# Rows of running sums fetched on GpSimd's queue instead of SyncE's, in a two-layer hybrid SSD and attention kernel

## The chip, the cores and the metric

The kernel runs on one core of one Trainium2 chip. The metric is the device time of one execution in microseconds (us), the median of several runs. An instruction that starts a DMA stands in the stream of the engine whose queue carries it: SyncE (SP) has no arithmetic and is used as a queue only, while GpSimd (POOL) both computes and issues.

## The reference, cut to what matters

Two layers of a parallel-branch block over 256 latent and 256 context tokens, model width 1024. Per layer:

```python
u_l = modulate(rmsnorm(xl, norm1_w[i]), sh1_l, sc1_l) @ w_in[i]     # and u_c for the context
ys  = ssd_branch(...)          # bidirectional Mamba-2 scan, 16 heads, chunks of 128 tokens
ya  = diff_attn_branch(...)    # differential attention, 8 heads
xl  = xl + g1_l * branch_merge(ys_l, ya_l, gate_l, w_br_ssd[i], w_br_att[i], w_out[i])
xl  = xl + g2_l * conv_ffn(h_l, w_up[i], ffn_conv_w[i], ffn_conv_b[i], w_down[i])
```

The part around the change is the scan inside a chunk, for each head and each of two directions:

```python
a_cs     = jnp.cumsum(a, axis=-1)              # running sums of dt * a_head
decay_in = jnp.exp(segsum(a))                  # exp(a_cs[l] - a_cs[s])
y_diag   = jnp.einsum('bgcls,bgrcls,bcsgrp->bclgrp', cb, decay_in, xd)
y_off    = jnp.einsum('bclgn,bcgrpn,bgrcl->bclgrp', cc, h_in, jnp.exp(a_cs))
```

## The kernel before, in words

All weights are float32 and stream from DRAM once per use. Tiles of 128 x 4 x 256 (`raw`, three buffers, 512 KB each) are loaded by `load_w` (L304) on SP's queue. ScalarE (ACT) rounds each to a high part `whi` (L313), VectorE (DVE) takes the remainder `wlo` (L314), three buffers each, and TensorE (PE) makes three matmuls of them (L393 to L395, L407 to L409). The order of instructions on each engine is chosen at build time by a scheduler from its own estimates; only attention and scan matmuls are pinned in program order. On the chip every engine works through its stream strictly in that order.

The scan's work is woven into the big matmuls: generators `states` and `outputs` (one of each for every group g of four heads) are advanced a step at a time by `pump` while the matmuls of xs (L1019 to L1021), the gates and z are emitted. The running sums are computed once per layer, and written by eight small DMAs to the DRAM tensor `csd` (L861). `outputs` then needs, for chunk t and group g, the sums of four heads and two directions spread over all 128 partitions. This is the tile `cs` (128 x 2 x 4 x 128, two buffers), which `fetch` (L950) fills with one broadcast DMA: rows of 2 KB from `csd`, the same to every partition, 512 KB in all. There are 16 fetches in layer 0 (four chunks) and 8 in layer 1 (two chunks), 24 together.

From a fetched `cs`, `head` makes what the chunk's matmuls need, in this order: ACT takes cc = exp(cs) (L966); POOL subtracts the column sums in place, once for each direction (L969, twice); DVE takes the minimum of the two directions (L972); ACT takes its exponential, E (L974); DVE multiplies cc by C (L975). Later DVE multiplies X by E (L993), which is the last reader of the `cs` buffer. A fetch for chunk t + 2 into the same buffer can go once that L993 is done. The first two fetches of a layer have no earlier `cs`: they wait for the memory of the attention branch, which is free when the last matmul of the GEMM with `w_br_att` has read `yah` (pmmmm<-yah,wlo).

POOL's other work here is `xd` (L925), the decayed inputs of the state matmuls `psstate` (L930). PE takes these in program order, so that everything behind one in PE's stream waits for it. xs of head pair j comes from two PSUM banks (`mm`) by a convolution (`conv3`: L568 on ACT, L571 and L572 on DVE), a tanh (L665) and a product (L666); PE then transposes xs (psssT). A bank can be written again after its L572.

```python
raw = fetch(0)
nxt = head(0, raw)
if NT > 1: raw = fetch(1)
for t in range(NT):
    ...                       # X of chunk t, times E (L993)
    if t + 1 < NT: nxt = head(t + 1, raw)
    if t + 2 < NT: raw = fetch(t + 2)
    ...                       # pyyd matmuls of chunk t
```

Of the kernel before, what the change touches and what calls it, by code (L numbers as in the profile page):

```python
# [59 lines left out]
def hybrid_backbone_kernel(  # L60
# [6 lines left out]
    nc = tc.nc  # L67
    V, A, G, T = nc.vector, nc.scalar, nc.gpsimd, nc.tensor
# [7 lines left out]
    def nm(s):  # L76
        cnt[0] += 1
        return f"{s}_{cnt[0]}"

    def bank(tag, what=""):  # L80
        return psp.tile([P, 512], F32, tag=tag, name=nm("p" + tag + what), bufs={"mm": 2, "s": 3, "y": 2, "m": 1}[tag])


    def pmm(*a, **k):
        return tc.keep_in_program_order(T.matmul(*a, **k))  # L85
# [489 lines left out]
    for i in range(DEPTH):  # L575
# [41 lines left out]
        if i == 0:  # L617
# [5 lines left out]
            for f in range(4):  # L623
# [10 lines left out]
                for cc in range(2):  # L634
                    for fb in range(2):
                        cs = slice(fb * P, fb * P + P)
# [182 lines left out]
        if True:  # L819
# [28 lines left out]
            for dr in range(2):  # L848
                cs = slice(16 * dr, 16 * dr + 16)
# [94 lines left out]
        def outputs(g, sh):  # L944
            while "xT" not in sh:
                yield None
            xT, h_in = sh["xT"], sh["h"]
            yb = [bank("y", "yd"), bank("y", "yd")]

            def fetch(t):  # L950
                cs = up.tile([P, 2, 4, P], F32, tag="cs", name=nm("cs"), bufs=2)
                nc.sync.dma_start(cs.rearrange("p d h l -> p d (h l)"),
                                  csd[t, :, 4 * g:4 * g + 4, :].rearrange("d h l -> d (h l)").partition_broadcast(P))
                return cs

            def head(t, cs):
                tsl = slice(t * P, (t + 1) * P)
                cb = bank("s", "cb")
                pmm(cb[:, 0:P], BF[g][:, tsl], CF[g][:, tsl], start=True, stop=True)
                cbm = up.tile([P, 2, P], F32, tag="cbm", name=nm("cbm"), bufs=2)  # L960
                V.tensor_tensor(cbm, cb[:, 0:P].unsqueeze(1).to_broadcast([P, 2, P]), tri2, op=ALU.mult)

                cc = up.tile([P, 2, 4, P], F32, tag="cc", name=nm("cc"), bufs=2)
                dirs = [dr for dr in range(2) if not (dr == 0 and t == 2) and not (dr == 1 and t == 3)]
                d0, d1 = dirs[0], dirs[-1] + 1
                A.activation(cc[:, d0:d1], cs[:, d0:d1], AF.Exp)  # L966

                for dr in range(2):
                    G.tensor_tensor(cs[:, dr], cs[:, dr],  # L969
                                    csc[:, t, 16 * dr + 4 * g:16 * dr + 4 * g + 4].unsqueeze(2).to_broadcast([P, 4, P]),  # L970
                                    op=ALU.subtract)
                V.tensor_tensor(cs[:, 0], cs[:, 0], cs[:, 1], op=ALU.min)  # L972
                E = cs[:, 1]
                A.activation(E, cs[:, 0], AF.Exp)  # L974
                V.tensor_tensor(cc[:, d0:d1].rearrange("p d h l -> p (d h) l"), cc[:, d0:d1].rearrange("p d h l -> p (d h) l"),  # L975
                                CF[g][:, tsl].unsqueeze(1).to_broadcast([P, 4 * (d1 - d0), P]), op=ALU.mult)
                return cbm, cc, E, dirs

            raw = fetch(0)
            yield 1  # L980
            nxt = head(0, raw)
            if NT > 1:
                raw = fetch(1)
            yield 1
            for t in range(NT):
                tsl = slice(t * P, (t + 1) * P)
                cbm, cc, E, dirs = nxt
                X = up.tile([P, 4, P], F32, tag="X", name=nm("X"), bufs=2)
                for h in range(4):
                    dcol = [dtT[:, t, 16 * dr + 4 * g + h:16 * dr + 4 * g + h + 1] for dr in range(2)]  # L990
                    A.activation(X[:, h, :], cbm[:, 0, :], AF.Copy, scale=dcol[0])
                    V.scalar_tensor_tensor(X[:, h, :], cbm[:, 1, :], dcol[1], X[:, h, :], op0=ALU.mult, op1=ALU.add)
                V.tensor_tensor(X, X, E, op=ALU.mult)  # L993
                yield 1
                if t + 1 < NT:
                    nxt = head(t + 1, raw)
                    yield 1
                if t + 2 < NT:
                    raw = fetch(t + 2)
                while "done" not in sh:  # L1000
                    yield None
                for f in range(2):
                    for h in (2 * f, 2 * f + 1):
                        r = slice(64 * (h % 2), 64 * (h % 2) + 64)
                        pmm(yb[f][r, tsl], xT[:, t, h * 64:(h + 1) * 64], X[:, h, :], start=True, stop=False)
                    for dr in dirs:
                        for h in (2 * f, 2 * f + 1):
                            r = slice(64 * (h % 2), 64 * (h % 2) + 64)
                            pmm(yb[f][r, tsl], h_in[dr, t][:, h * 64:(h + 1) * 64], cc[:, dr, h, :],
                                start=False, stop=dr == dirs[-1])  # L1010
                yield 1
            for f in range(2):
                j = 2 * g + f
                V.scalar_tensor_tensor(xs[j][:, 0:N], xs[j][:, 0:N], L["D"][:, j:j + 1], yb[f][:, 0:N],
                                       op0=ALU.mult, op1=ALU.add)
            done.append(g)
            yield 1
# [189 lines left out]
```

## Time and profile before

| | us |
|---|---|
| median of 3 runs (1746.28 to 1748.42) | 1747.45 |
| the profiled execution | 1740.01 |
| its span, first to last instruction | 1738.2 |
| PE busy in it | 1667.1 (96%) |
| DVE busy | 1148.0 (66%) |
| ACT busy | 848.2 (49%) |
| POOL busy | 181.3 (10%) |
| mean granted TensorE clock | 0.993 of full speed |

Rows of the profile name an engine, a line of the kernel, the operation and its tiles as output<-input. In a timeline a row starts with its start and its length in us, and ends with the idle time ahead of it and what ended that, in square brackets. In a list of waits the three numbers are the total, the number of waits and the longest. In a table of stretches the columns are the length, the busy time and count of each engine, the granted clock (PEclk, 1.00 is full speed), the share of the DMA engines and GB/s.

### The profile page before, as it was taken

Reading aid. Unit: us, or ns where it says so; the run is one execution under the profiler, and the core shown is the slowest. Engines: PE = TensorE matmul, PEld = TensorE weight load, DVE = VectorE, ACT = ScalarE, POOL = GpSimd, SP = SyncE. Lnnn points to the kernel's source line nnn. Section 1 sums busy time; section 2 is a strip of 40 time slices with the busy share of each in tenths; the row PEclk is TensorE's granted clock in tenths of the full one; section 3 lists DMA queues with packets and bytes.
Section 4 is the critical chain, followed back from the end, with each engine's and each line's share of the span. In section 5 each row is a group of like instructions: output and inputs, shape, how many; then the busy total and the mean of one; then the engine's idle time right before and its main releaser. Section 6 shows DMA issues by size and latency. Waiting matters only on the chain. (4 is left out here: it accounts for less than half of the span.)

```text
span 1738.2 us, 27022 instructions
## 1 busy us (share of the span) xinstructions
PE 1667.1 (96%) x10547; PEld 1406.2 (81%) x10547; DVE 1148.0 (66%) x2008; ACT 848.2 (49%) x1567; POOL 181.3 (10%) x212
## 2 busy tenths in 40 slices
PE   7999999999988999999999999999999898989997
PEld 4788878777766788888888888788879788989997
DVE  4776667325988855766666326666675789779964
ACT  3565665413545423644444225555655455466653
POOL 3000010001433000300000002100000252010000
PEclk9999999999999999999999999999999999989999
DMA  9644333555443234233323335844535445646653
GB/s 317 215 127 126 115 119 108 166 173 146 121 107 100 74 109 146 74 97 97 97 87 95 92 108 161 255 146 146 152 93 171 121 110 144 199 154 185 193 176 117
DMA packets 233199, 240.71 MB, mean 138 GB/s; under 512 B 10908, under 2 KB 223551, under 8 KB 233071
## 3 DMA queue, kind: packets, MB, share of 16 engines
q1 hardware_dynamic: 230720, 237.14, 45.4%
q8 instruction: 83, 1.36, 0.3%
q0 software_dynamic: 1312, 1.03, 0.2%
q10 hardware_dynamic: 1039, 0.81, 0.1%
q14 instruction: 45, 0.37, 0.1%
HBM read 234.62 MB, written 4.33 MB: 137 GB/s over the span
## 5 line engine op out<-in xcount | busy, mean ns | idle before, releaser
L314 DVE TENSOR_TENSOR wlo<-raw,whi 128x1024 fp32r<-128x1024 f32 (+1 forms) x318 | 388.3, 1221 | 255.7 <-ACT whi L313 254.8
L313 ACT CAST whi<-raw 128x1024 fp32r<-128x1024 f32 (+1 forms) x318 | 329.2, 1036 | 378.4 <-PE pmmmm L408 146.6
L407 PE MATMUL pmmmm<-th,whi 128*128 128x512 f32 x744 | 306.3, 412 | 1.6 <-DVE chv L572 1.6
L408 PE MATMUL pmmmm<-tl,whi 128*128 128x512 f32 x744 | 296.5, 399 | 0.0
L409 PE MATMUL pmmmm<-th,wlo 128*128 128x512 f32 x744 | 295.6, 397 | 0.0
L407 PEld LDWEIGHTS pmmmm<-th,whi 128*128 128x128 f32 x744 | 140.5, 189 | 42.2 <-issue 7.9
L409 PEld LDWEIGHTS pmmmm<-th,wlo 128*128 128x128 f32 x744 | 140.4, 189 | 34.5 <-issue 1.0
L408 PEld LDWEIGHTS pmmmm<-tl,whi 128*128 128x128 f32 x744 | 140.5, 189 | 31.0 <-issue 2.2
L393 PE MATMUL pmmmm<-th,whi 128*128 128x256 f32 x480 | 138.5, 289 | 1.5 <-ACT whi L313 1.3
L395 PE MATMUL pmmmm<-th,wlo 128*128 128x256 f32 x480 | 134.7, 281 | 0.6 <-DVE wlo L314 0.6
L394 PE MATMUL pmmmm<-tl,whi 128*128 128x256 f32 x480 | 134.8, 281 | 0.0
L969 POOL TENSOR_TENSOR cs<-cs,csc 128x512 f32<-128x512 f32 x48 | 69.1, 1454 | 264.0 <-DMA cs<-csd 141.5
L393 PEld LDWEIGHTS pmmmm<-th,whi 128*128 128x128 f32 x480 | 90.7, 189 | 6.2 <-issue 3.8
L394 PEld LDWEIGHTS pmmmm<-tl,whi 128*128 128x128 f32 x480 | 90.8, 189 | 0.7 <-issue 0.4
L395 PEld LDWEIGHTS pmmmm<-th,wlo 128*128 128x128 f32 x480 | 90.6, 189 | 0.8 <-DVE wlo L314 0.8
L409 PE MATMUL psmm<-th,wlo 128*128 128x512 f32 x200 | 79.3, 397 | 0.0
L725 ACT ACTIVATE e<-psscore,nmx 128x512 f32<-128x512 f32 (+1 forms) x96 | 58.1, 610 | 43.5 <-DVE nmx L722 40.5
L408 PE MATMUL psmm<-tl,whi 128*128 128x512 f32 x200 | 79.2, 396 | 0.0
L521 POOL TENSOR_TENSOR rs<-ms,mhalf 128x2 f32<-128x2 f32 x9 | 6.3, 699 | 698.5 <-DVE ms L518 698.5
L407 PE MATMUL psmm<-th,whi 128*128 128x512 f32 x200 | 79.0, 395 | 0.0
L722 DVE TENSOR_REDUCE nmx<-psscore 128x1 f32<-128x512 f32 (+1 forms) x80 | 51.8, 684 | 34.3 <-PE psscore L85 34.2
L441 PE MATMUL pmmmm<-whi,th 128*128 128x256 f32 x256 | 74.3, 290 | 0.0
(346 smaller groups left out, 3899.0 us busy)
## 6 DMA issues: line engine op xcount, KB each, us to landing
raw<-in_w_in_dram SPq DMA_DIRECT2D x124, 512.0 KB, 4.0
raw<-in_w_up_dram SPq DMA_DIRECT2D x88, 512.0 KB, 3.6
mraw<-in_w_mod_dram SPq DMA_DIRECT2D x80, 512.0 KB, 4.7
raw<-in_w_down_dram SPq DMA_DIRECT2D x45, 512.0 KB, 3.6
cs<-csd SPq DMA_DIRECT2D x24, 512.0 KB, 5.8
boot<-in_w_mod_dram SPq DMA_DIRECT2D x16, 512.0 KB, 9.3
raw<-in_w_br_att_dram SPq DMA_DIRECT2D x16, 512.0 KB, 3.6
raw<-in_w_br_ssd_dram SPq DMA_DIRECT2D x16, 512.0 KB, 3.5
```

The costliest lines, as they stand in the source:

```text
L313: pin(A.copy(hi[:, 0:n, :], raw[:, 0:n, :]))
L314: pin(V.tensor_tensor(lo[:, 0:n, :], raw[:, 0:n, :], hi[:, 0:n, :].bitcast(F32), op=ALU.subtract))
L393: T.matmul(o[f], whi[:, kk, cs], xh, start=first, stop=False)
L394: T.matmul(o[f], whi[:, kk, cs], xl, start=False, stop=False)
L395: T.matmul(o[f], wlo[:, kk, cs], xh, start=False, stop=last)
L407: T.matmul(o, whi[:, k % 4, cs], hi[k][:, 0:n], start=k == 0, stop=False)
L408: T.matmul(o, whi[:, k % 4, cs], lo[k][:, 0:n], start=False, stop=False)
L409: T.matmul(o, wlo[:, k % 4, cs], hi[k][:, 0:n], start=False, stop=k == k_tiles - 1)
L441: T.matmul(b[:, n, :], hi[k][:, ts], whi[:, k % 4, :], start=k == 0 and n == 0, stop=False)
L722: V.tensor_reduce(nmx[:, cc, 0:ng], sc[cc].rearrange("p (g k) -> p g k", g=ng), axis=AX.X, op=ALU.max, negate=True)
L725: A.activation(e[cc][:, g * w:(g + 1) * w], sc[cc][:, g * w:(g + 1) * w], AF.Exp, bias=nmx[:, cc, g:g + 1], accum_out=sm[:, cc, g:g + 1])
L969: G.tensor_tensor(cs[:, dr], cs[:, dr], csc[:, t, 16 * dr + 4 * g:16 * dr + 4 * g + 4].unsqueeze(2).to_broadcast([P, 4, P]), op=ALU.subtract)
```

## The change

One line: the DMA in `fetch` is issued by GpSimd (`G`) instead of SyncE.

```diff
             def fetch(t):
                 cs = up.tile([P, 2, 4, P], F32, tag="cs", name=nm("cs"), bufs=2)
-                nc.sync.dma_start(cs.rearrange("p d h l -> p d (h l)"),
+                G.dma_start(cs.rearrange("p d h l -> p d (h l)"),
                                   csd[t, :, 4 * g:4 * g + 4, :].rearrange("d h l -> d (h l)").partition_broadcast(P))
                 return cs
```

SP's stream loses its 24 fetches, and otherwise keeps its order. POOL's stream gains them, and the scheduler, which now counts on the fetches at other times, puts some work of ACT, DVE, PE and POOL in another order near them. Three places matter below. In the pieces, a minus marks a row that stands there before and a plus one that stands there now.

First, ACT at the start of the scan of layer 0. `cs_4044` and `cs_4067` are the first two fetched tiles, `chv_3939` is the convolution of the first half of xs, `whi_3979` and `whi_3997` are the weights of the next matmuls.

```order
 L313 CAST whi_3909<-raw_3889 128x1024
-L568 ACTIVATE chv_3939<-pmmmm_3913,cols_157 128x512
-L665 ACTIVATE cth_3938<-chv_3939 128x512
-L313 CAST whi_3979<-raw_3895 128x1024
 L966 ACTIVATE cc_4060<-cs_4044 128x1024
 L966 ACTIVATE cc_4109<-cs_4067 128x1024
+L974 ACTIVATE cs_4044<-cs_4044 128x512
+L568 ACTIVATE chv_3939<-pmmmm_3913,cols_157 128x512
+L974 ACTIVATE cs_4067<-cs_4067 128x512
+L313 CAST whi_3979<-raw_3895 128x1024
+L665 ACTIVATE cth_3938<-chv_3939 128x512
+L313 CAST whi_3997<-raw_3977 128x1024
```

Both exponentials and the first E now stand ahead of the convolution of xs, which stood ahead of them.

Second, DVE at the same place.

```order
 L314 TENSOR_TENSOR wlo_3910<-raw_3889,whi_3909 128x1024
+L975 TENSOR_TENSOR cc_4060<-cc_4060,CF_0_617 128x1024
+L972 TENSOR_TENSOR cs_4044<-cs_4044 128x512
+L975 TENSOR_TENSOR cc_4109<-cc_4109,CF_0_617 128x1024
+L972 TENSOR_TENSOR cs_4067<-cs_4067 128x512
 L571 SCALAR_TENSOR_TENSOR chv_3939<-pmmmm_3913,cols_157,chv_3939 128x2x255
 L572 SCALAR_TENSOR_TENSOR chv_3939<-pmmmm_3913,cols_157,chv_3939 128x2x255
+L314 TENSOR_TENSOR wlo_3980<-raw_3895,whi_3979 128x1024
 L666 SCALAR_TENSOR_TENSOR xs_0_3874<-cth_3938,chv_3939 128x512
-L314 TENSOR_TENSOR wlo_3980<-raw_3895,whi_3979 128x1024
-L975 TENSOR_TENSOR cc_4060<-cc_4060,CF_0_617 128x1024
-L972 TENSOR_TENSOR cs_4044<-cs_4044 128x512
```

The four operations on the first two fetched tiles moved ahead of L571 and L572, which free the bank of `pmmmm_3913`. In layer 1 the second L966 and the first L972 and second L975 move ahead of the convolution in the same way; the first L966 and L975 stood ahead of it already.

Third, POOL in the middle of layer 0's scan, where the ninth and tenth fetch (`cs_4790`, `cs_4814`) are worked on.

```order
 L969 TENSOR_TENSOR cs_4645<-cs_4645,csc_622 128x512 x2
+L952 DMA cs_4790<-csd_623 128x2x512
 L925 TENSOR_TENSOR xd_4757<-xT_4566,ddt_624 128x256
+L952 DMA cs_4814<-csd_623 128x2x512
+L925 TENSOR_TENSOR xd_4786<-xT_4566,ddt_624 128x256
 L969 TENSOR_TENSOR cs_4790<-cs_4790,csc_622 128x512 x2
-L925 TENSOR_TENSOR xd_4786<-xT_4566,ddt_624 128x256
-L969 TENSOR_TENSOR cs_4814<-cs_4814,csc_622 128x512 x2
+L969 TENSOR_TENSOR cs_4814<-cs_4814,csc_622 128x512
 L925 TENSOR_TENSOR xd_4836<-xT_4566,ddt_624 128x256
+L969 TENSOR_TENSOR cs_4814<-cs_4814,csc_622 128x512
```

The ninth fetch now stands behind both subtractions on `cs_4645` (the eighth), while `xd_4786` moved ahead of two subtractions and `xd_4836` ahead of one. Further up in the same stream the eighth fetch stands behind the second subtraction on `cs_4573` (the seventh), and further down the twelfth (`cs_4964`) behind the first subtraction on the eleventh (`cs_4883`).

## The prediction

> **What bounds the kernel now.** PE is busy 96% of the span; I read a table of stretches over the two scans, then who waited for whom.
>
> ```profile
> 406.00:430.00 24.00, 21.74 (x123) 16.19 (x115) 15.37 (x17) 9.95 (x13) 6.68 (x6) 1.00 0.61 176
> 430.00:500.00 70.00, 67.48 (x417) 53.68 (x417) 62.75 (x113) 36.89 (x74) 26.84 (x26) 1.00 0.44 113
> 500.00:530.00 30.00, 23.51 (x140) 18.07 (x140) 21.11 (x35) 12.79 (x27) 14.13 (x12) 0.92 0.36 89
> 530.00:580.00 50.00, 44.20 (x274) 34.40 (x271) 44.69 (x82) 25.26 (x54) 12.66 (x13) 0.98 0.40 103
> 1346.00:1373.00 27.00, 22.35 (x98) 17.41 (x98) 16.24 (x19) 10.10 (x14) 7.23 (x6) 0.94 0.47 123
> 1373.00:1480.00 107.00, 100.95 (x776) 89.74 (x775) 94.44 (x168) 58.55 (x109) 37.83 (x35) 1.00 0.46 127
> ```
>
> The columns are length, busy time of PE, its weight loads, DVE, ACT and POOL, then the clock. The first four rows are layer 0's scan, the last two layer 1's. PE idles 2.3 + 2.5 + 6.5 + 5.8 = 17.1 us and 4.7 + 6.1 = 10.8 us. Where the clock stands under 1.00, time is lost too: 30 x 0.08 + 50 x 0.02 = 3.4 us and 27 x 0.06 = 1.6 us. So 33 us, 1.9% of the span, are the most that any change of the scans could win.
>
> ```profile
> PE psstate L85 <- POOL xd L925: 6.5, 4, 3.4
> ```
>
> ```profile
> ACT whi L313 <- PE pmmmm L408: 146.6, 92, 8.6
> ```
>
> ```profile
> SPq L952 <- DVE X L993: 83.7, 14, 11.3
> ```
>
> The first row is from PE's waits in layer 0's scan: the state matmuls wait for POOL. In the second, from the list of waits over the span, the rounding of the weights waits for PE to release a `whi` buffer, so weights lie ready. The third is SP's own queue: fetches wait there for the last reader of their buffer. From a queue of their own they go no earlier, as that reader is the same. Only the first pair of each layer can.
>
> **The change part by part.** The price of an issue and a landing:
>
> ```profile
> L952 SPq DMA_DIRECT2D cs<-csd x24: 360/367/460, 409.0 to 1447.0; - x24
> DMA to landing us min/median/max: 4.8/5.8/8.8
> ```
>
> ```profile
> L1156 POOL DMA_DIRECT2D fwb<-in_final_norm_w_dram x1: 615/615/615, 1510.3 to 1510.3; - x1
> DMA to landing us min/median/max: 6.1/6.1/6.1
> ```
>
> The second pair is the one broadcast of 512 KB that POOL issues already, and nearest to the new fetch: I take 0.6 us of POOL and 6.1 us to landing. Bounds of the landing: 4.8, the best `cs`, and 9, just over the worst.
>
> *Removed from SP*: 24 issues of 0.37 us and their waits. Weights may be issued earlier, but the `whi` row says that nobody waits for them: 0. Without that cover, what a fetch holds back on SP's queue, up to 11.3 us at a time, would be won.
>
> *A: start of layer 0.* The rows are of PE, SP, ACT (the one of layer 1 is for its length) and POOL, then the means of DVE's operations in the scan.
>
> ```profile
> 405.24 0.39 PE L408 MATMUL pmmmm<-yal,whi 128*128 128x512 f32 x1
> 405.47 0.40 PE L409 MATMUL pmmmm<-yah,wlo 128*128 128x512 f32 x1
> 419.18 0.50 PE L407 MATMUL pmmmm<-th,whi 128*128 128x512 f32 x1
> 426.88 0.66 PE L88 MATMUL psssT<-kt,xs 128*128 128x128 f32 x4 [2.10 <-DVE xs L666]
> 409.03 1.00 SPq L952 DMA_DIRECT2D cs<-csd  x2
> 1353.62 1.06 ACT L966 ACTIVATE cc<-cs 128x1024 f32<-128x1024 f32 x1 [6.07 <-DMA cs<-csd]
> 417.79 5.50 POOL L969 TENSOR_TENSOR cs<-cs,csc 128x512 f32<-128x512 f32 x4 [112.32 <-DMA cs<-csd]
> ```
>
> ```profile
> L314 DVE TENSOR_TENSOR wlo<-raw,whi 128x1024 fp32r<-128x1024 f32 x20 | 25.4, 1270 | 4.0 <-ACT whi L313 4.0
> L972 DVE TENSOR_TENSOR cs<-cs 128x512 f32<-128x512 f32 x16 | 13.0, 811 | 7.8 <-POOL cs L969 7.8
> L975 DVE TENSOR_TENSOR cc<-cc,CF 128x1024 f32<-128x1024 f32 x8 | 10.6, 1321 | 2.6 <-ACT cc L966 2.5
> L666 DVE SCALAR_TENSOR_TENSOR xs<-cth,chv 128x512 f32<-128x512 f32 x8 | 6.2, 772 | 1.8 <-ACT cth L665 1.5
> L571 DVE SCALAR_TENSOR_TENSOR chv<-pmmmm,cols,chv 128x510 f32<-128x510 f32 x8 | 5.9, 742 | 7.4 <-ACT chv L568 7.4
> L910 DVE COPY xT<-psssT 128x512 f32<-128x512 f32 x8 | 5.5, 682 | 0.0
> ```
>
> The memory is free when the matmul at 405.47 ends, at 405.9. POOL has nothing else queued, so the pair goes 3.1 us earlier, and the first lands at 405.9 + 6.1 = 412.0. But this work now stands ahead of the convolution L568, which before went as soon as PE had filled its bank. Step by step:
>
> - ACT's first cc takes 1.06: 413.1. POOL's four subtractions take 5.5, to 418.7, the first two half of that, to 415.9.
> - DVE: first minimum 0.8, to 416.7; second cc product 1.3, to 418.0; second minimum after POOL, 418.7 to 419.5; only then L571 and L572, 0.74 each: the bank is free at 421.0. PE wants it at 419.18 and idles 1.8.
> - `wlo_3980` 1.3 and L666 0.8 put the first xs at 423.1. PE gets to its transposition after six matmuls (0.23 each, by the first two rows; 1.4), at 422.4, and idles 0.7.
> - The second xs follows by 1.3 + 1.5 + 0.7 + 0.8 = 4.3, at 427.4 instead of 426.88. Its transposition also stands five matmuls earlier in PE's stream, which are 5 x 0.23 = 1.2 us still to do. PE is 0.5 + 1.2 = **+1.7 us** late.
>
> A second landing up to 415.2 doesn't count: POOL is busy with the first until 415.9.
>
> What the idling does to PE's clock:
>
> ```profile
> 513.13 0.70 PE L85 MATMUL psstate<-xd,bT 128*128 128x256 f32 x2 [3.41 <-POOL xd L925]
> 527.48 0.70 PE L85 MATMUL psstate<-xd,bT 128*128 128x256 f32 x2 [2.63 <-POOL xd L925]
> ```
>
> These two waits lie in the stretch of clock 0.92 and ahead of that of 0.98; the wait of 2.10 at 426.88 lies in one of 1.00. So a fall costs 3.4 / 2 = 1.7 us and comes somewhere above 2.1 us of idling. With 2.5 in two pieces it may go either way: half, **+0.8**. On the other hand DVE, busy 90% of 430 to 500 and nearest to a second bound there, is little later than before, so part of PE's lateness is taken back in waits for X: **-0.8**, half of the 1.7, and at most the 2.5 us that PE idles in that row. Bounds of A: 0 (landing at 4.8) and +6 (landing at 9: all of it 2.9 later, and the fall).
>
> *B: POOL's queue in mid layer 0.*
>
> ```profile
> 479.82 5.31 SPq L952 DMA_DIRECT2D cs<-csd  x2
> 495.38 4.83 SPq L952 DMA_DIRECT2D cs<-csd  x2
> 486.86 1.03 POOL L969 TENSOR_TENSOR cs<-cs,csc 128x512 f32<-128x512 f32 x1
> 508.26 4.06 POOL L969 TENSOR_TENSOR cs<-cs,csc 128x512 f32<-128x512 f32 x2 [2.30 <-ACT cc L966]
> ```
>
> The eighth fetch (second of the first row, 484.8) now waits behind a subtraction on the seventh, which ended at 487.9 and will end some 0.8 later with a landing of 6.1. The ninth (495.4) waits behind both subtractions on the eighth: 488.7 + 6.1, an exponential and two subtractions of 1.0, about 497. So its chain is 1.6 late, and with it the tenth's subtractions. On both of these `xd_4836` waited when PE idled 3.41; it now waits for one (2.0 less): 1.6 - 2.0, about **-0.3**. Queued behind the waiting fetches are `xd` tiles. PE waited for 4 of the 24 of layer 0, by the row of `psstate`; the others have slack, which hides the 0.6 of an issue. Bounds: -3.7 (chain not late and no fall: 2.0 + 1.7), +2.
>
> *C:* the wait of 2.63 is for an `xd` whose xT copy stood behind L972 on DVE and now stands ahead: **-0.8**, one L972 (bounds -2.5 without the fall, and 0).
>
> *D: end of layer 0.*
>
> ```profile
> 564.10 0.37 SPq L952 DMA_DIRECT2D cs<-csd  x1
> 569.34 0.63 ACT L966 ACTIVATE cc<-cs 128x512 f32<-128x512 f32 x1 [0.88 <-DMA cs<-csd]
> 575.51 0.44 PE L85 MATMUL pyyd<-X,xT 128*64 128x128 f32 x4 [1.73 <-DVE X L993]
> ```
>
> The last fetch is on the path to a wait of PE: 6.1 to landing instead of 5.2 is **+0.9**.
>
> *E: start of layer 1.*
>
> ```profile
> 1346.66 0.37 SPq L952 DMA_DIRECT2D cs<-csd  x1
> 1349.30 0.46 SPq L952 DMA_DIRECT2D cs<-csd  x1
> 1359.37 0.47 PE L407 MATMUL pmmmm<-th,whi 128*128 128x512 f32 x1 [1.58 <-DVE chv L572]
> 1363.96 0.63 PE L88 MATMUL psssT<-kt,xs 128*128 128x128 f32 x4 [2.94 <-DVE xs L666]
> ```
>
> Here the first cc (the ACT row in A) stands in front already, and waited 6.07 us. The first fetch goes when it went, the second 2 us earlier. From 1354.7: two subtractions 2.8, minimum 0.8, product 1.3, L571, minimum, L572 (2.3) give the bank at 1361.9, 2.5 later; the first xs, after `wlo` and L666, comes at 1364.0, as now. The idling falls into one piece and the slow clock begins earlier, so less of it is left after the transposition: **-0.4**, bounds -2 and +3. The other six fetches land with time to spare.
>
> Sum: 1.7 + 0.8 - 0.8 - 0.3 - 0.8 + 0.9 - 0.4 = **+1.1 us**. The profiled execution took 1740.01 us, 1.8 around its span, and would take 1741.1. The median of the runs shown lies 7.4 higher, at 1747.45; I add the difference there: **1748.5 us**. A measurement of this kernel can tell about 0.2% (3.5 us) from no change.
>
> **The rivals.** *Faster:* the chain in B is not late, the waits of 3.41 and 2.63 shrink and the clock falls at neither. With A taken back wholly: -3.7 - 2.5 + 0.9 - 0.4 = -5.7, 1741.8 us. For it: `xd_4786` and `xd_4836` do go ahead. Against: the eighth fetch is 3.9 us late by its place alone.
>
> *Slower:* fetches made by POOL land late, because POOL's part in them is held up by DVE.
>
> ```profile
> L969 POOL TENSOR_TENSOR cs<-cs,csc x48: 1031/1319/2108, 417.8 to 1457.3; 128x512 f32<-128x512 f32 x48
> ```
>
> POOL's subtractions stretch from 1.03 to 2.11 us beside DVE's work. With landings of 9 us, A is +6, B +2, C 0, D +2.9 more, E +3: 15 at most, and +7 when half of it shows, 1754.5 us. It decides from a landing of about 7.5 us. Against: 6.1 in the one row of its kind, where DVE is busy too. The Trainium skill's page "SBUF — State Buffer", section "SBUF: two separate sides", states such a rule against this change: while DVE runs a copy in a two-port mode, GpSimd can't write descriptors and the transfer stands. Its section "Who interferes with whom" has copies and casts within SBUF do it, but not tensor_tensor; in the rows of DVE in A the one copy, L910, reads PSUM, so no run here shows the rule at work.
>
> The Trainium skill's page "DMA: Bandwidth & Descriptors", section "Specifications", puts the first byte at about 1 us on GpSimd's path and 0.6 on the others: 0.4 per landing, an estimate by which D would be +0.4 and the sum +0.6.
>
> *Nothing at all:* A is taken back and B to E cancel: 1747.5, inside the forecast.
>
> **How the numbers follow.** Forecast, with the last rival in it: 0.48, its own range 1744 to 1751. Faster: 0.20. Slower: 0.32, more than faster, since A stands on the written order and the gains on slack. 1742 to 1756.5 reaches to the faster rival and past the slower's half price, and leaves about 2 in 10 out.
>
> **What would show it.** Right: the first L966 of layer 0 near 412 and its L568 after L972; PE idle about 2 us ahead of the first L407 after 419; landings near 6; an `xd` wait near 510 still there. Wrong: landings over 7.5, or a clock of 1.00 from 500 to 530.

## The result, and the profile after

| | median us | runs | range |
|---|---|---|---|
| before | 1747.93 | 4 | 1746.28 to 1749.42 |
| after | 1758.27 | 4 | 1756.47 to 1759.20 |

The ratio is 1.0058 (95% interval 1.0041 to 1.0076): the change made the kernel 10 us slower, between 7 and 13. The prediction was +1.1; the measured time lies 1.8 us above the upper end of its range. Below, a ratio is turned into us by the median of before beside it, some 1745 us.

The profiled execution of after took 1759.17 us with a span of 1757.4, and that is 19.2 more than the span shown of before. To see where, I take the same rows of DVE in both traces, those of L314, which makes the rounding rest of the weights (`wlo`, 318 of them, most with the row of a wait ahead), and subtract a row's start before from its start after. The column "second pair" does it with another pair of executions, `after_again` and `before_again` of the runs below:

```
start before   after less before   second pair   place
      393.5           2.3              1.7        ahead of layer 0's scan
      436.5           6.3              6.0        first convolutions done
      465.8           6.9              6.6
      492.8           9.2              9.2
      530.9          11.5             12.4
      598.6          12.7             12.2        layer 0's scan done
     1343.8          15.8             10.6        ahead of layer 1's scan
     1410.4          16.9             10.5        start of layer 1's scan done
     1721.0          19.0              8.6        end
```

Both pairs lose 10.5 us in layer 0's scan (2.3 to 12.7, 1.7 to 12.2): 4 at its start, 6 behind it. Outside, the pairs disagree, +3.1 and -1.6 between the scans, +2.1 and -1.9 behind 1410; that is the executions' own, as two profiled executions of the kernel before show it, too (first experiment). So the question is layer 0's scan, and some 0 to 1 us at layer 1's start.

The same stretches as in the table of the prediction, from the first pair (they begin later by the shift); length, then busy time of PE, its loads, DVE, ACT and POOL, then the clock:

```profile
408.30:436.30 28.00, 23.58 (x122) 17.91 (x115) 14.36 (x17) 9.91 (x14) 9.38 (x9) 0.88 0.54 151
436.30:509.00 72.70, 68.88 (x411) 54.81 (x410) 64.44 (x111) 36.70 (x74) 32.07 (x33) 0.98 0.40 108
509.00:541.20 32.20, 25.77 (x152) 20.13 (x153) 24.77 (x38) 13.30 (x29) 14.06 (x15) 0.89 0.35 85
541.20:592.70 51.50, 43.60 (x260) 34.14 (x259) 45.54 (x82) 24.95 (x53) 15.68 (x17) 0.93 0.38 100
1361.80:1390.00 28.20, 22.46 (x99) 17.82 (x98) 14.95 (x19) 10.45 (x14) 9.37 (x9) 0.88 0.45 117
```

In the four rows of layer 0 PE is busy 161.8 us instead of 156.9 and idle 22.6 instead of 17.1. So half of the loss is idling, 5.5 us, and half, 4.9 us, is PE being busy longer with about the same matmuls (945 instead of 954), which goes with the slow clock: it is under 1.00 in all four rows, before in two. What PE waited for in layer 0's scan (us in total, times, longest):

```profile
PE pyyd L85 <- DVE X L993: 12.6, 5, 5.0
PE psstate L85 <- POOL xd L925: 3.6, 2, 2.4
PE pmmmm L407 <- DVE chv L572: 2.7, 1, 2.7
PE pmmod L465 <- DMA mraw<-in_w_mod_dram: 1.7, 1, 1.7
PE pscb L85 <- DVE h L938: 1.5, 1, 1.5
```

The waits for `xd` fell (6.5 before), those for X grew (8.2 before), and two at the start are new. The longest wait for X, 5.0 us at 554.85, is not the change's alone: `before_again` has one of 4.08 in its place, the first trace of before one of 2.12. The fetch's own group on POOL, with who waited for it:

```profile
L952 POOL DMA_DIRECT2D cs<-csd x24: 727/751/791, 408.7 to 1464.8; - x24
...
who waited for it (us, times):
  ACT cc L966: 35.3, 13
  POOL cs L969: 31.7, 8
...
DMA to landing us min/median/max: 5.0/5.9/9.9
```

An issue takes 0.75 us of POOL, and the median landing, 5.9 us, is the 5.8 of before. ACT waits for it 35.3 us in all, 21.8 before: apart from the pairs, the fetches do not travel longer, they start late.

**The start of layer 0.** Its rows after; the first is PE's last matmul on the memory that the pair goes into:

```profile
407.74 0.40 PE L409 MATMUL pmmmm<-yah,wlo 128*128 128x512 f32 x1
...
408.70 1.60 POOL L952 DMA_DIRECT2D cs<-csd  x2 [100.96 <-PE pmmmm L409]
...
410.73 0.82 SPq L463 DMA_DIRECT2D mraw<-in_w_mod_dram  x1
...
416.01 1.06 ACT L966 ACTIVATE cc<-cs 128x1024 f32<-128x1024 f32 x1 [7.03 <-DMA cs<-csd]
...
419.49 1.06 ACT L966 ACTIVATE cc<-cs 128x1024 f32<-128x1024 f32 x1 [2.42 <-DMA cs<-csd]
...
420.63 3.20 POOL L969 TENSOR_TENSOR cs<-cs,csc 128x512 f32<-128x512 f32 x2 [0.41 <-ACT cc L966]
...
422.80 0.64 PE L465 MATMUL pmmod<-mraw,s 128*32 128x256 f32 x8 [1.72 <-DMA mraw<-in_w_mod_dram]
423.86 0.69 DVE L972 TENSOR_TENSOR cs<-cs 128x512 f32<-128x512 f32 x1 [0.93 <-POOL cs L969]
424.47 0.74 DVE L571 SCALAR_TENSOR_TENSOR chv<-pmmmm,cols,chv 128x510 f32<-128x510 f32 x1
...
425.25 0.75 DVE L572 SCALAR_TENSOR_TENSOR chv<-pmmmm,cols,chv 128x510 f32<-128x510 f32 x1
...
426.14 0.77 PE L407 MATMUL pmmmm<-th,whi 128*128 128x512 f32 x1 [2.70 <-DVE chv L572]
```

The chain is the one foreseen, fetch, exponential, subtractions, minimum, convolution, PE; but it runs over the second fetch of the pair, which lands at 419.5, 9.9 us after its issue. And one wait is of another kind: the second `mraw` load, issued at 410.73, is now behind the pair instead of ahead of it, and PE waits 1.72 us for it.

**The first long wait behind it.** X of the fourth chunk ends at 473.53, and with it the sixth fetch's buffer is free:

```profile
472.85 0.68 DVE L993 TENSOR_TENSOR X<-X,cs 128x512 f32<-128x512 f32 x1
...
475.95 1.04 POOL L969 TENSOR_TENSOR cs<-cs,csc 128x512 f32<-128x512 f32 x1
...
476.93 0.75 POOL L952 DMA_DIRECT2D cs<-csd  x1
...
482.79 1.06 ACT L966 ACTIVATE cc<-cs 128x1024 f32<-128x1024 f32 x1 [3.77 <-DMA cs<-csd]
483.75 0.62 ACT L665 ACTIVATE cth<-chv 128x512 f32<-128x512 f32 x1
484.27 1.27 ACT L991 ACTIVATE X<-cbm,dtT 128x128 f32<-128x128 f32 x4
487.93 0.68 DVE L993 TENSOR_TENSOR X<-X,cs 128x512 f32<-128x512 f32 x1
...
488.67 0.64 PE L85 MATMUL pyyd<-X,xT 128*64 128x128 f32 x4 [3.23 <-DVE X L993]
```

The fetch stands in POOL's list behind a subtraction and an `xd`, and goes at 476.93, 3.4 us after that X. It lands 5.8 us later. ACT stands at its exponential for 3.77 us, and behind that in ACT's own list are the copies (L991) for the X that PE needs next. So a late fetch reaches PE through two lists, POOL's and ACT's. Before, the same fetch went at once after its X (467.51), and PE waited 0.40 us at this place:

```profile
465.98 1.53 DVE L993 TENSOR_TENSOR X<-X,cs 128x512 f32<-128x512 f32 x1
```

```profile
467.57 0.37 SPq L952 DMA_DIRECT2D cs<-csd  x1
```

```profile
479.81 0.44 PE L85 MATMUL pyyd<-X,xT 128*64 128x128 f32 x4 [0.40 <-DVE X L993]
```

### The profile page after: what moved, and what is told of

Read it like the earlier page. It is cut to its first block, busy times and chain, and to the rows that moved or that the text cites. A ratio compares the mean times of both kernels' runs of the same rounds, so it can differ in the third digit from the quotient of the medians.

```text
span 1757.4 us, 26996 instructions
## 1 busy us (share of the span) xinstructions
PE 1675.5 (95%) x10547; PEld 1411.7 (80%) x10547; DVE 1152.7 (66%) x2008; ACT 848.6 (48%) x1567; POOL 199.8 (11%) x236
## 5 line engine op out<-in xcount | busy, mean ns | idle before, releaser
L314 DVE TENSOR_TENSOR wlo<-raw,whi 128x1024 fp32r<-128x1024 f32 (+1 forms) x318 | 387.6, 1219 | 257.9 <-ACT whi L313 256.8
```

The lines of the kernel that those rows point to most:

```text
L314: pin(V.tensor_tensor(lo[:, 0:n, :], raw[:, 0:n, :], hi[:, 0:n, :].bitcast(F32), op=ALU.subtract))
```

## The experiments

Two theories, and a third that the prediction had as its slower rival:

- **Order theory:** the loss comes from the order that the scheduler writes for ACT and DVE once it sees the pair go early: the head's work ahead of the convolution.
- **Queue theory:** it comes from where the fetches stand: later ones behind work in POOL's list, the pair ahead of loads of weights.
- **Transfer theory:** what GpSimd issues lands later, or slows other transfers.

There are fourteen runs; ratios are to runs of before on the same chip.

| kernel | ratio | 95% interval | us |
|---|---|---|---|
| `before_again` | 0.9995 | 0.998 to 1.001 | -0.9 |
| `after_again` | 1.0067 | 1.0051 to 1.0084 | +11.7 |
| `pool_old_order` | 1.0037 | 1.0025 to 1.0049 | +6.5 |
| `sp_new_order` | 1.0038 | 1.0022 to 1.0053 | +6.6 |
| `first_old_order` | 0.9997 | 0.9981 to 1.0013 | -0.5 |
| `rest_old_order` | 1.0038 | 1.0024 to 1.0051 | +6.6 |
| `pool_hand_order` | 1.0018 | 1.0003 to 1.0033 | +3.1 |
| `pool_three_old_order` | 1.0005 | 0.9992 to 1.0017 | +0.9 |
| `sp_new_l0` | 1.0024 | 1.0011 to 1.0037 | +4.2 |
| `sp_new_l1` | 1.0010 | 0.9999 to 1.0022 | +1.7 |
| `sp_three_old_order` | 0.9948 | 0.9934 to 0.9961 | -9.1 |
| `three_rest_old_order` | 0.9976 | 0.9965 to 0.9988 | -4.2 |
| `sp_tiny_old_order` | 0.9995 | 0.9982 to 1.0008 | -0.9 |
| `sp_three` | 0.9965 | 0.9951 to 0.9979 | -6.1 |

### Both kernels again

`before_again` has no edit:

> The kernel before once more, unchanged: how far do two profiled executions of one program differ? Its profiled execution before took 1740.0 us, 7.4 below the median of its runs, and the two profiled executions compared so far differ by 19.2 us where the medians differ by 10.3. All theories expect a ratio of 1.000. If the difference outside the two scans is the execution's own, this profile shows some of it too (PE waiting for mraw loads between 1095 and 1130 us, a start some 2 us later); if it is the change's, this profile looks like the first one to 1 us there.

Ratio 0.9995. Its profiled span is 1745.8 us, 7.6 over the first one's 1738.2, by the same comparison of `wlo` starts: 1.3 of it before 105 us, 1.2 between the scans around 1120, 1.0 at layer 1's start, and 3.8 from 1410 on. Over layer 0's scan as a whole the two executions agree to 0.3 us, though not inside it: up to 531 the second wins 1.4 us on the first, and loses it again behind. So differences of a few us outside the scans, and of 1 to 2 us at one place inside them, are one execution's own, and what a pair of traces shows there is not put down to the change.

`after_again` has the one edit of the change:

> The changed kernel once more, beside the three others on one chip: +10 us over before (7 to 13), with some 9 to 10 us of it inside layer 0's scan and 1 to 3 in layer 1's.

+11.7 us (8.9 to 14.7); 10.5 in layer 0's scan as the table above shows, none in layer 1's start.

### Queue and order taken apart

The order of every engine's list is kept by dependencies that only order and never wait, from each instruction to the next of its engine. The list is written from the program of the kernel before, or of the changed one, and the fetches on POOL go where the scheduler puts them between the pinned instructions:

```
+KEEP = [
+    """
...
+""",
+]
+
+def keep(tc, nc):
+    at = {i.name: i for i in nc.cur_bb.bb.instructions}
+    for row in KEEP:
...
+        for a, b in zip(ids, ids[1:]):
+            tc.add_manual_dep(at[b], a, mybir.DependencyInfo(
+                mybir.DependencyClass.NoSync, mybir.DependencyReason.DATA), reason="keep")
...
         hybrid_backbone_kernel(tc, *args)
+        keep(tc, nc)
```

`pool_old_order` is the changed kernel with the lists of before:

> The fetches on GpSimd's queue as in the changed kernel, but the instructions of PE, DVE, ACT and POOL in the very order of the kernel before (the fetches go into POOL's list where the scheduler puts them). Order theory (the loss comes from the head's work written ahead of the convolution at the start of each layer): the loss at the starts goes, some 5 of the 10 us, and what is left is +3 to +5. Queue theory (the loss comes from where the fetches stand: behind subtractions in POOL's list, and the first pair ahead of loads of weights on the DMA engines): +8 to +11, as now. Transfer theory (what GpSimd issues lands later or slows other transfers): also +8 to +11, with landings of fetches or weights longer than before.

`sp_new_order` is the kernel before with the lists of the changed one:

> The opposite: the fetches on SyncE's queue as before, but PE, DVE, ACT and POOL in the very order of the changed kernel. Order theory: +5 to +8, with PE idle 4 to 6 us ahead of the first convolution's bank in each layer. Queue theory and transfer theory: -1 to +2.

Each has half: +6.5 (4.4 to 8.6) and +6.6 (3.8 to 9.3), together 13.1 where both at once gave 11.7 and 10. Keeping an order costs nothing by itself: `first_old_order` and `sp_tiny_old_order` below do it, too, and are at -0.5 and -0.9. Neither theory alone holds, and the expectations of neither were met for both: what the order theory gave for its own run came true, and what was left by the queue was more than it allowed. In the trace of `sp_new_order` PE idles at the two starts, in one piece each:

```profile
PE pmmmm L407 <- DVE chv L572: 6.5, 1, 6.5
```

```profile
PE pmmmm L407 <- ACT cs L974: 5.9, 1, 5.9
```

The first is layer 0's, the second layer 1's. By `wlo` starts against the first trace of before, less the difference ahead of the scan (so here and below), it is 5.6 us late at 436, and 4.1 at the end of layer 0's scan: 1.5 is taken back. In `pool_old_order` the start costs 1.4, and then it loses 2.4 by 493 and another 2.4 by the scan's end.

### The order, by layer

The same lists, the changed one's for one layer and those of before for the other:

> The fetches on SyncE's queue; the changed kernel's order on all engines in layer 0, the order of the kernel before in layer 1. By the profile with the changed order in both layers, layer 0 ended 4.1 us late (5.6 at its start, 1.5 taken back) and layer 1's start cost another 2.4: +3 to +5 here, with PE idle some 6.5 us ahead of the first convolution's bank of layer 0. If the order's +7 comes from elsewhere than the two starts, less than +2.

> The opposite: the changed kernel's order in layer 1 alone. By the same profile +2 to +3, with PE idle 5.6 to 5.9 us in one piece at layer 1's start instead of 1.5 and 2.9 in two.

+4.2 us (1.9 to 6.5) and +1.7 (-0.2 to 3.8): layer 0's share is as expected; layer 1's wait is there, 5.9 us in one piece instead of two of 1.4 and 3.0, but its price is not told from nothing.

### The queue, by fetches

```
-                G.dma_start(cs.rearrange("p d h l -> p d (h l)"),
+                (G if g == 0 and t < 2 else nc.sync).dma_start(cs.rearrange("p d h l -> p d (h l)"),
```

and the opposite, `(nc.sync if g == 0 and t < 2 else G)`; both with the lists of before.

> Order of the kernel before on all engines; only the first pair of fetches of each layer is on GpSimd's queue, the other six or fourteen on SyncE's. Theory of the loads (the pair goes 2.5 us earlier and so ahead of the second mraw load, for which PE then waits 2.2 us in the run with all fetches on GpSimd's queue): that wait stays, +1 to +2 us in all. Theory of POOL's list (what costs is a later fetch that stands behind other work of POOL): -0.5 to +0.5. If every fetch from GpSimd costs alike, 4 of 24 of +7: +1.2, and no wait for mraw.

> The opposite: the first pair of each layer on SyncE's queue, the rest on GpSimd's, order of the kernel before. Theory of POOL's list: +4 to +6, with the wait of 3 us for an X near 482 still there. Theory of the loads: +1 or less there, since no mraw load is overtaken. Cost by fetch: 20 of 24 of +7, +5.8, spread over both layers (some 4 us in layer 0, 1.5 in layer 1).

-0.5 us (-3.3 to 2.3) for the pair and +6.6 (4.2 to 8.9) for the rest: the whole of the queue's part is in the later fetches. The theory of the loads was right on its wait and wrong on its price. In `first_old_order` PE's one wait at the start is this, and in `rest_old_order` this:

```profile
PE pmmod L465 <- DMA mraw<-in_w_mod_dram: 1.8, 1, 1.8
```

```profile
PE psssT L88 <- DVE xs L666: 2.1, 1, 2.1
```

The wait for `mraw` comes in the place of the wait for `xs` that the kernel before has there: it delays PE, and the convolution catches up meanwhile. In this trace 1.0 us is lost at the start all the same, as the clock falls there; the median shows no loss.

### Three late fetches moved ahead

With the lists of before, the sixth, eighth and twelfth fetch of layer 0 went 3.5, 1.9 and 3.2 us after their X. POOL's list is now given with the fetches in it, and these three stand one or two places further ahead; the first of the three:

```
 L969 TENSOR_TENSOR cs_4492<-cs_4492,csc_622 128x512
+L952 DMA cs_4516<-csd_623 128x2x512
 L925 TENSOR_TENSOR xd_4488<-xT_4238,ddt_624 128x256
 L969 TENSOR_TENSOR cs_4492<-cs_4492,csc_622 128x512
-L952 DMA cs_4516<-csd_623 128x2x512
```

> All fetches on GpSimd's queue, order of the kernel before, and three of layer 0's sixteen fetches (the sixth, the eighth and the twelfth, which went 3.5, 1.9 and 3.2 us after the last reader of their buffer) moved one or two places ahead in POOL's list, in front of a subtraction or an xd; nothing else is changed. Theory of POOL's list: these go within 1 us of the last reader, PE's wait of 3.2 us near 482 falls under 1, and +7 becomes +2 to +4. Theory of POOL's time (24 issues of 0.75 us) and of slower transfers: +6 to +8, as before the move.

+3.1 us (0.5 to 5.8): as the theory of POOL's list had it, though the wait fell to 1.34 and not under 1. The sixth fetch goes at 468.59 where it had gone at 472.94 in `pool_old_order`, 0.8 us after its X, and the twelfth 0.5 after its own; the eighth still goes 1.7 late, behind a subtraction on the seventh, which has to land first. PE's wait of 3.22 us near 484 is now this:

```profile
468.59 0.75 POOL L952 DMA_DIRECT2D cs<-csd  x1
```

```profile
481.01 0.44 PE L85 MATMUL pyyd<-X,xT 128*64 128x128 f32 x4 [1.34 <-DVE X L993]
```

The traces alone show less than the medians. By `wlo` starts this one loses 1.5 us from 436 to 493, where `pool_old_order` loses 2.4, and 5.1 by the scan's end, where that one loses 6.1. At the start, where nothing was moved, it loses nothing instead of 1.4.

Is the rest POOL's time? `sp_tiny_old_order` leaves the fetches on SyncE's queue and puts an issue of 4 KB in each place where POOL's list had one, so that it has POOL's time and no coupling:

```
+                tiny = up.tile([P, 8], F32, tag="tiny", name=nm("tiny"), bufs=8)
+                G.dma_start(tiny, konst[:, 0:8])
```

> The kernel before, in its own order, with the fetches on SyncE's queue; at each place where the changed queue would have a fetch in POOL's list stands an issue of a tiny load (128 x 8 numbers of a constant, that nobody reads) instead. It waits for nothing and moves almost nothing, so it costs POOL's time alone. Theory of lists (an issue hurts by being late behind POOL's work, and by holding POOL's work back while it waits for its buffer): -1 to +2. Theory of POOL's time: +3 to +5, what was left of +7 when the three late fetches had been moved ahead.

```profile
L953 POOL DMA_DIRECT2D tiny<-in_konst_dram x24: 547/577/607, 407.2 to 1440.8; - x24
```

24 issues of 0.58 us are there, 13.9 us of POOL, and the time is -0.9 us (-3.1 to 1.4): nothing of them shows. A fetch's issue takes 0.17 us more; no run tests that part alone. What is left of the queue's part is therefore most likely the coupling, or the landing, told below.

### A third buffer

The fetch waits for the X of two chunks before, as `cs` has two buffers. With three it waits for the X of three chunks before, and can go a chunk earlier:

```
-                cs = up.tile([P, 2, 4, P], F32, tag="cs", name=nm("cs"), bufs=2)
+                cs = up.tile([P, 2, 4, P], F32, tag="cs", name=nm("cs"), bufs=3)
```

On GpSimd's queue, lists of before:

> All fetches on GpSimd's queue, order of the kernel before on PE, DVE, ACT and POOL's own work, but three buffers for cs, so that a fetch waits for a reader one tile earlier and the wait is over when POOL comes to it. Theory of POOL's list: the waits for X and xd that late fetches made go, but three transfers instead of two now stand ahead of the mraw load at the start, where PE waits 3 to 5 us: 0 to +4 in all. POOL's time or slower transfers: +6 to +8.

+0.9 us (-1.4 to 3.0) on the kernel before, as the theory of POOL's list had it, though PE now waits 2.1 and 3.5 us for `mraw` at the start. By `wlo` starts it is 5.5 us late at 436 and 2.1 at the scan's end, so it wins 3.4 us on the kernel before in between. That pointed to a version better than both; on SyncE's queue, and with the first three fetches there and the rest on GpSimd's:

> The fetches on SyncE's queue, the order of the kernel before, but three buffers for cs. With fetches on GpSimd's queue the third buffer lost 5.5 us at the start (loads overtaken) and had won 3.5 of it back by 530 us, against two buffers on SyncE's queue. Here no mraw load is overtaken. If that gain is the third buffer's: -2 to -4, with the waits for xd near 510 and 525 (3.0 and 1.7 us) at half or less. If it was only the taking back of a late start: -1 to +1.

> Three buffers, the first three fetches of each layer on SyncE's queue, the rest on GpSimd's, order of the kernel before. If POOL's list costs only through late fetches, and the third buffer makes lateness harmless: the same as three buffers on SyncE's queue alone, -2 to -4. If an issue of 0.75 us on POOL costs by itself: 1 to 3 us more than that one.

-9.1 us (-11.5 to -6.8) on SyncE's queue, more than expected, and -4.2 (-6.1 to -2.1) with most fetches on GpSimd's. So the third buffer does not make GpSimd's queue harmless. With three buffers that queue costs 10 us, +0.9 against -9.1, where it cost 6.5 with two: 5 of them are the later fetches, by the -4.2, and 5 the first three, by the waits for `mraw`. The third buffer's own gain only hid that in `pool_three_old_order`. A fetch on POOL still goes 0.3 to 0.8 us after its X there, two of them 2.4 us.

I had put such a difference down to the issue's time beforehand, and the tiny issues speak against that. The trace shows the list's other side. In `three_rest_old_order` the eleventh fetch waits at the head of POOL's list for its buffer, whose X ends at 500.97. The ninth chunk's subtractions, which stand behind it, could have begun when ACT's exponential was done, at 500.8, and begin at 502.27 (the profile names an ACT row for the fetch's wait, which is the last that ended before it):

```profile
501.50 0.75 POOL L952 DMA_DIRECT2D cs<-csd  x1 [3.29 <-ACT gs L1028]
502.27 2.04 POOL L969 TENSOR_TENSOR cs<-cs,csc 128x512 f32<-128x512 f32 x2
```

```profile
499.75 1.05 ACT L966 ACTIVATE cc<-cs 128x1024 f32<-128x1024 f32 x1
```

With all fetches on SyncE's queue the same exponential ends at 498.45, and the subtractions begin at once:

```profile
498.52 3.12 POOL L969 TENSOR_TENSOR cs<-cs,csc 128x512 f32<-128x512 f32 x2 [4.88 <-ACT cc L966]
```

So a fetch in POOL's list is held up by POOL's work, and holds up POOL's work. How much of the 4.9 us between the two runs that is, no run here tells. Where the third buffer's gain comes from, by one stretch of `before_again` and the same of `sp_three_old_order`:

```profile
501.00:530.00 29.00, 24.30 (x146) 18.96 (x147) 21.15 (x35) 12.83 (x27) 14.17 (x12) 0.88 0.31 91
```

```profile
499.00:523.00 24.00, 21.41 (x146) 16.68 (x141) 21.02 (x35) 11.22 (x25) 13.84 (x12) 1.00 0.42 110
```

In each, 146 matmuls ran, in 5 us less with the third buffer: 2.1 less idling, and 2.9 less because the clock no longer falls (1.00 instead of 0.88).

Last, the one word alone, with the scheduler's own order:

> The kernel before with three buffers for cs instead of two and nothing else: no order is given, the scheduler writes its own, which moves an exponential or a product by a place here and there in mid layer 0 and leaves the starts alone. Three buffers in the given order were 10 us faster than before. If that comes from the buffers and not from the order: -7 to -12.

-6.1 us (-8.6 to -3.7), just short of what was expected. Two buffers against three is the cause. The kept order may be worth up to 3 us more, though the two intervals overlap; why, was not tried.

## Why the prediction was wrong

The forecast was that POOL's list has slack, so that 1 us of cost remained. It has slack for the time of an issue, and none for its place. Two steps failed, the landing of the second fetch in A and the search for late fetches in B; beside them the order, which the prediction had read rightly, cost more than it said. By the prediction's own steps:

- **The price:** right. 0.75 us an issue instead of 0.6, 5.9 to landing instead of 6.1; and an issue's time, by the tiny loads, costs nothing.
- **Removed from SP, 0:** right as a sum. Not all weights lay ready: the pair overtakes a load of `mraw`, and PE waits 1.7 us for it. That wait only takes another's place.
- **A, start of layer 0, +1.7:** the chain was right, the size was not: 4.0 in the trace. The step that failed is "A second landing up to 415.2 doesn't count". It landed at 417.2 on the clock of before (419.5 less the shift of 2.3), since the pair went 0.6 after PE's last matmul and the second took 9.9 us. The prediction had priced both with the 6.1 of a single broadcast, though the pair of before, at 8.8 the slowest landing it quoted, was the nearer one. The clock fell (**+0.8**, half, was 1.8: PE is busy 23.58 us instead of 21.74). That a fall comes "somewhere above 2.1 us of idling" doesn't hold: see the last point below. Of the **-0.8** taken back nothing shows in the table; with the order alone, 1.5 of 5.6 is.
- **B, -0.3:** wrong in sign, and the largest error. From 466 to 531 the changed kernel loses 4.6 us (5.8 in the second pair), with C in it. The step's own sum is short: 488.7 + 6.1, an exponential and two subtractions of 1.0 make 497.8 and not 497, which alone turns -0.3 into some +0.5. The step looked for a late fetch only where PE had already waited for an `xd`, and found the eighth. The sixth is 3.4 us late and reaches PE by way of ACT's list and X; the twelfth is 3.6 late. That "the others have slack, which hides the 0.6 of an issue" was true of the issue and beside the point: what counts is not how long an issue takes but where it stands. That the queue's part lies in the later fetches is shown (+6.6 against -0.5). That it is their lateness is shown for one wait, 3.22 to 1.34; for the whole it is likely, as the intervals with and without the move, 0.5 to 5.8 and 4.4 to 8.6, overlap.
- **C, -0.8:** right in kind. The wait of 2.63 near 525 is one of 1.14 now; in the second pair it is 1.72 and 1.14.
- **D, +0.9:** +1.3 in one pair, -0.2 in the other: not told from the executions' own.
- **E, -0.4:** +1.1 and -0.1; the order alone +1.7 (-0.2 to 3.8). The idling did fall into one piece, 5.64 us, but PE's bank came at 1363.4 on the clock of before (1379.2 less the shift of 15.8), not 1361.9:

```profile
1377.73 0.69 DVE L972 TENSOR_TENSOR cs<-cs 128x512 f32<-128x512 f32 x1 [0.28 <-POOL cs L969]
1378.35 0.74 DVE L572 SCALAR_TENSOR_TENSOR chv<-pmmmm,cols,chv 128x510 f32<-128x510 f32 x1
```

```profile
1379.23 0.77 PE L407 MATMUL pmmmm<-th,whi 128*128 128x512 f32 x1 [5.64 <-ACT cs L974]
```

L572 frees the bank at 1379.09, behind the minimum on the second fetch; the exponential that the profile names ended 0.06 later. The second fetch, 9.5 us from issue to landing, is the same step as in A.

- **The rivals:** "Slower" was to come from landings over 7.5 us; they are at 5.9. The result is on that side by a mechanism that no rival had: the coupling of two lists. The signs named in advance came true (a landing near 6, L568 behind the first L972, an `xd` wait near 510 still there, of 2.4 us), apart from "about 2 us" of idling, which was 4.4, and the first L966 "near 412", which was at 413.7 on the clock of before. They showed the steps that were thought of, and none of them was for a late fetch.

Open is what the remaining 3 us of `pool_hand_order` consist of: the eighth fetch, still 1.7 us late, the others, which are 0.3 to 0.8 late, fetches that hold up subtractions, or later landings. No run here separates these.

## What to carry to other kernels

A transfer that waits for a buffer is better not issued from an engine that computes: it is late by whatever stands ahead of it in that list, and can hold back what stands behind it, and neither shows in its own duration. For each such transfer, go through the engine's list and compare the time of its turn with the time at which its buffer is free, and follow the consumer's list to the bound engine. Let the wait end earlier (here a third buffer, -6 to -9 us) and leave the queue where it is: with that buffer, too, the move cost 10 us. Price a burst by a burst.

## What the runs showed of the hardware

- **A burst of two lands far later than one.** The two broadcasts of 512 KB that go together took 6.9 and 8.8 us from SyncE and 7.2 and 9.9 from GpSimd, single ones around 5.5; three at once, 7.2, 10.4 and 13.7 in `pool_three_old_order`. PE waits for loads issued behind them as well, 1.7 us for `mraw` in after. The Trainium skill's page "DMA: Bandwidth & Descriptors", section "Issuing engines are not separate DMA queues", says that transfers of all issuing engines run on the same 16 engines and interleave; the runs agree, as that load of SyncE's comes late behind a pair of GpSimd's.
- **From GpSimd a single fetch lands a little later.** With two buffers, the 14 later fetches of layer 0 took 5.4 to 5.6 us on the mean of each run from GpSimd; from SyncE 5.2 to 5.5, by the five to nine whose landing the trace has. In layer 1 it is 6.2 to 6.6 against 5.5 to 5.6 (three landings a run; 6.1 by the two of `first_old_order`). The prediction's estimate of 0.4, from the Trainium skill's page "DMA: Bandwidth & Descriptors", section "Specifications", lies between the two differences. The rule of the Trainium skill's page "SBUF — State Buffer", section "SBUF: two separate sides", by which a DVE copy in a two-port mode keeps GpSimd from writing descriptors, shows in none of these landings: no single fetch of after took over 7.0 us.
- **Whether a piece of idling slows the clock hangs on where it lies.** In after the clock falls to half at 423.9, inside the second of two idle pieces of 1.7 and 2.7 us with 0.6 us of matmuls between them, and stays there 6.8 us. The rows of after, 4 us each:

```profile
424.00:428.00 4.00, 1.86 (x5) 1.50 (x6) 3.72 (x6) 3.36 (x5) 0.00 (x0) 0.50 0.00 0
428.00:432.00 4.00, 4.00 (x15) 3.28 (x14) 3.81 (x6) 0.99 (x2) 0.00 (x0) 0.66 0.70 183
```

In `first_old_order` it falls after a single piece of 1.84 us. The wait of 2.10 us for `xs`, ahead of 426.88 in before, stands in seven traces: the clock falls behind it in `rest_old_order`, `sp_new_l1` and `sp_tiny_old_order`, and not in `before`, `before_again`, `sp_three_old_order` and `three_rest_old_order`. In each trace the falls begin whole multiples of 3.41 us apart, and those inside the two scans last 3.41, 6.83 or 10.24 us. So a wait of some 2 us can only be priced with a chance, as the prediction did with its half, and two traces can differ by a fall without any difference in the kernel.
